# Gates and up-projections with the tokens stationary, the output projection in two halves of its k-tiles, and the memory pools moved to opposite ends

## The chip, the cores and the metric

One core of a Trainium2 chip runs the whole layer. Times are device microseconds of one execution; the profile is that of one execution of its own.

## What is computed

One decoder layer over 256 tokens of width 2048, in float32. A combined input projection feeds three attention branches (indexer-selected, block-gated, cross-attention into 256 memory tokens). Their outputs go through up-projections, are weighted by sigmoid gates, summed and projected; then come a layer norm, a mixture of 32 experts (two for each token), and a second layer norm.

```python
g_a, g_b, g_c = jnp.split(jax.nn.sigmoid(h @ w_gate[l] + b_gate[l]), 3, axis=-1)
merged = g_a * (o_a @ w_up_a[l]) + g_b * (o_b @ w_up_b[l]) + g_c * (o_c @ w_up_c[l])
x = layer_norm(ALPHA * x + merged @ w_o[l], ln1_g[l], ln1_b[l])
y = hier_moe(x, w_grp[l], b_grp[l], w_rt[l], b_rt[l], w1[l], w3[l], w2[l])
x = layer_norm(ALPHA * x + y, ln2_g[l], ln2_b[l])
```

`w_gate` is 2048 x 6144, `w_o` 2048 x 2048, and each of the 32 experts has three matrices of 2048 x 512.

## The kernel before

**Dense part.** `proj` (line 167) makes a list of units. A unit is one 128x512 (or two 128x256) piece of a weight matrix, 256 KB: `ld` loads it into one of six staging slots of `stt`, `sp` splits it on ScalarE and VectorE into a high and a low float32r part `wh`, `wl` (`split`, lines 147 and 148; three buffers), and `run` does three matmuls for each piece, high by high, high by low, low by high. `emit` (line 580) issues the load five units ahead and the split two units ahead. In the form "W" the weights stand in the array and the 256 tokens stream (12 matmuls of 256 columns a unit, lines 199 to 202; the result has channels on partitions). In the form "S" the tokens stand and the weights stream (6 matmuls of 512 columns, lines 207 to 209; the result has tokens on partitions). The instructions of an engine are put in an order by a scheduler, by when it reckons them ready.

The stages in order: input projections with the attention heads as filler between them, six gate stages of 32 units (form W, filler in the first three; `gate_evac` adds the bias, a value per partition, on ScalarE), 64 units of up-projections (W; `up_evac` multiplies by the gate, adds the branches and splits the sum into the tiles `mg`), 64 units of the output projection (S), over five column pieces `WO`, each over all 16 k-tiles. After a piece `residual_sum` adds it to the residual in `wx`, and `logit_step` transposes the sum and multiplies it with the router.

**Memory and stream.** `Stream` (line 636) loads the expert weights in slots of 2 MB. The first eight keys are loaded in halves: eight half-loads during the last gates, eight more at the units `WOL` of the output projection. After the dense part two further slots, `acc` and `yb`, open for one load each, and `wx` when the normalised rows have been taken from it. In the steady part `hidden` (line 987) uses four slots at a time and `used` gives them back, whereupon the next loads are issued on SyncE's queue.

**Tail.** The last group of four experts has its `w2` cut by output columns (`LAST`: 1024, 512, 512), so that the second norm can begin on the first columns. `load_ln2` spreads the norm's two rows over all partitions into the slot `main.ln` by 32 matmuls and eight ScalarE copies; it stands after the last group's `hidden`. Then comes a branch (`tc.If`), and in its `Else` the last slices (`last_slices`, line 1082) and `fast_tail` (line 1135), which prefills PSUM with the bias row, finishes the statistics and writes eight pieces of 128x512.

Of the kernel before, what the change touches and what calls it, by code (L numbers as in the profile page):

```python
# [8 lines left out]
F32 = mybir.dt.float32  # L9
# [40 lines left out]
def hybrid_trunk(ctx: ExitStack, tc: tile.TileContext, xp, xT, memT, w_mem_kv, w_in, gq, gkv, g_kidx, b_kidx,  # L50
# [21 lines left out]
    cs1 = ph1.enter_context(tc.tile_pool(name="cs1", bufs=1))  # L72
    gq_s = cs1.tile([P, 4], F32, name="gq_s")
    gkv_s = cs1.tile([P, 2], F32, name="gkv_s")
    bg_s = cs1.tile([P, 48], F32, name="bg_s")
# [9 lines left out]
    def load_consts():  # L85
# [4 lines left out]
        nc.sync.dma_start(bg_s, bg)  # L90
        nc.sync.dma_start(g1p, ln1_gp)
# [12 lines left out]
    xm = ph1.enter_context(tc.tile_pool(name="xm", bufs=4))  # L104
    wsp = ph1.enter_context(tc.tile_pool(name="wsp", bufs=3))
    wks = ExitStack()
    wk = wks.enter_context(tc.tile_pool(name="wk", bufs=2))
    k2 = ctx.enter_context(tc.tile_pool(name="k2", bufs=1, side="right"))
    slots = [k2.tile([P, W2D], F32, name=f"wk{i}") for i in range(NSK)]
    mos = ExitStack()  # L110
    g8 = mos.enter_context(tc.tile_pool(name="g8", bufs=6, side="right"))
    mo = mos.enter_context(tc.tile_pool(name="mo", bufs=4, side="right"))
# [37 lines left out]
    def act_tiles(pool, nm):  # L150
        ts = [pool.tile([P, 8, T], F32R, name=f"{nm}{n}", tag="a") for n in ("H0", "L0", "H1", "L1")]
        return Act(ts[0::2], ts[1::2], 8)
# [14 lines left out]
    def proj(src, c0, n, act, nkt, kind, evac, last=False):  # L167
# [7 lines left out]
        for u in range(nu):  # L175
            def ld(u=u):
                st = state["s", u] = stg()
                R["ld"] = nc.sync.dma_start(st[:, :kp * n].rearrange("p (k n) -> p k n", k=kp),
                                  src[u * kp * P:(u + 1) * kp * P, c0:c0 + n].rearrange("(k p) n -> p k n", p=P))
# [6 lines left out]
            def mm(u=u, cs=(0, 1)):  # L186
# [4 lines left out]
                for k in range(kp):  # L191
                    wh, wl = (t[:, k * n:(k + 1) * n] for t in state[u])
                    kt = u * kp + k
                    st_, sp_ = kt == 0, kt == nkt - 1
# [36 lines left out]
    A["x"] = act_tiles(xm, "x")  # L231
# [9 lines left out]
    wi = wk.tile([P, 2, NIH], F32, name="wi", bufs=1)  # L241
    later = []
# [125 lines left out]
    for k, i in enumerate(GO):  # L368
        proj_cols(w_gate, i * 1024, 1024, X, NKT, "W",
# [917 lines left out]
```

## Time and profile before

| what | us |
|---|---|
| median of 3 runs | 1702.85 (1702.12 to 1704.21) |
| the profiled execution's own time | 1701.77 |
| its span in the profile | 1700.0 |
| dense part, start to end of the output projection | 0 to 757 |
| routing and first gather | 757 to 767 |
| experts, up to the last weight's landing | 767 to 1673 |
| after the last landing | 1673 to 1700 |

The times in the profile count from the start of the span. Busy shares are of one engine; a matmul's duration in the profile is a latency, and what matmuls cost in a row is the distance from one start to the next.

### The profile page before, as it was taken

What the parts mean: (1) busy time and instruction counts of PE and PEld (TensorE: products, weight loads), DVE (VectorE), ACT (ScalarE), POOL (GpSimd) and SP (SyncE); (2) the same over time, 40 slices, a digit from 0 to 9 for tenths busy, and PEclk for the clock granted to TensorE, in tenths of its full rate; (3) what the DMA queues carried; (4) which work ended last, traced back from release to release, by engine and by line L of the source; (5) the groups of instructions that cost most, each with busy time, mean ns of one, the idle gap of its engine ahead of it and who ended that gap; (6) DMA issues with size and microseconds to landing.
All of it is one profiled execution on the core that took longest, in us unless ns stands there. A gap on an engine that the chain in (4) does not pass through costs nothing.

```text
span 1700.0 us, 23691 instructions
## 1 busy us (share of the span) xinstructions
PE 1472.8 (87%) x9489; PEld 956.8 (56%) x9489; DVE 596.2 (35%) x1126; ACT 465.0 (27%) x873; POOL 13.0 (1%) x24
## 2 busy tenths in 40 slices
PE   9999999999999999997976967877758768768677
PEld 8989989999999998883321222312212213222122
DVE  6656765565454676551120210200200101001004
ACT  5545455676545444441100000000000000000011
POOL 0000000000000000010000000000000000000000
PEclk9999999999999999998987978978979879879779
DMA  7766665555776667949999999999999999999994
GB/s 237 229 187 165 163 164 160 156 156 163 273 265 210 184 186 262 316 148 424 426 427 426 428 427 427 427 428 426 427 428 426 427 427 427 427 427 427 428 404 158
DMA packets 118279, 540.70 MB, mean 318 GB/s; under 512 B 13680, under 2 KB 27792, under 8 KB 93072
## 3 DMA queue, kind: packets, MB, share of 16 engines
q1 hardware_dynamic: 118160, 539.10, 82.8%
q8 instruction: 77, 1.26, 0.3%
q14 instruction: 42, 0.34, 0.1%
HBM read 536.95 MB, written 2.10 MB: 317 GB/s over the span
## 4 chain that ended last, share of the span: by engine, by line
PE 55%; DMA 41%; DVE 1%; ACT 1%; issue 1%; SPq 1%; POOL 0%; ACTq 0%; DVEq 0%; POOLq 0%
DMA wg<-in_w_dram 17%; DMA wk<-in_w_dram 15%; PE ps L202 10%; PE ps L199 10%; PE ps L201 10%; PE h L992 8%; DMA wkk<-in_w_dram 5%; DMA wx<-in_w_dram 4%; PE ps L208 3%; PE ps L207 3%; PE ps L209 3%; PE yp L1073 3%; PE yp L1096 1%; DMA stt<-in_w_o_dram 1%; SPq L704 1%
## 5 line engine op out<-in xcount | busy, mean ns | idle before, releaser
L148 DVE TENSOR_TENSOR wl<-stt,wh 128x512 fp32r<-128x512 f32 (+1 forms) x492 | 333.9, 684 | 264.1 <-ACT wh L147 260.5
L147 ACT CAST wh<-stt 128x512 fp32r<-128x512 f32 (+1 forms) x492 | 300.7, 615 | 311.1 <-PE ps L201 203.8
L992 PE MATMUL h<-wg,xg 128*32 128x512 f32 x912 | 240.4, 702 | 80.2 <-DMA wg<-in_w_dram 80.2
L199 PE MATMUL ps<-xH,wh 128*128 128x256 f32 x1024 | 293.7, 287 | 0.0
L202 PE MATMUL ps<-xH,wl 128*128 128x256 f32 x1024 | 289.7, 283 | 0.8 <-DVE wl L148 0.7
L201 PE MATMUL ps<-xL,wh 128*128 128x256 f32 x1024 | 289.7, 283 | 0.0
L992 PE MATMUL h<-wk,xg 128*32 128x512 f32 x688 | 201.9, 712 | 57.3 <-DMA wk<-in_w_dram 57.3
L199 PEld LDWEIGHTS ps<-xH,wh 128*128 128x128 f32 x1024 | 196.2, 192 | 1.6 <-issue 1.3
L202 PEld LDWEIGHTS ps<-xH,wl 128*128 128x128 f32 x1024 | 196.1, 192 | 1.5 <-DVE wl L148 1.5
L201 PEld LDWEIGHTS ps<-xL,wh 128*128 128x128 f32 x1024 | 196.3, 192 | 0.3
L963 DVE TENSOR_SCALAR xg<-gp,g1n,b1n 128x128 f32<-128x128 f32 x56 | 23.0, 410 | 428.2 <-PE h L992 375.3
L992 PEld LDWEIGHTS h<-wg,xg 128*32 128x32 f32 x912 | 53.1, 126 | 198.0 <-DMA wg<-in_w_dram 108.8
L992 PE MATMUL h<-wkk,xg 128*32 128x512 f32 x208 | 116.9, 718 | 18.3 <-DMA wkk<-in_w_dram 18.3
L992 PEld LDWEIGHTS h<-wk,xg 128*32 128x32 f32 x688 | 44.5, 128 | 148.7 <-DMA wk<-in_w_dram 83.0
L992 PE MATMUL h<-wx,xg 128*32 128x512 f32 x208 | 115.7, 710 | 12.1 <-DMA wx<-in_w_dram 12.1
L960 ACT ACTIVATE xg<-gp,b1n,g1n 128x128 f32<-128x128 f32 x56 | 25.6, 457 | 361.1 <-PE h L992 252.4
L1073 PE MATMUL yp<-wg,yb 128*32 128x512 f32 x368 | 95.8, 597 | 8.3 <-DMA wg<-in_w_dram 8.3
L1073 PE MATMUL yp<-wk,yb 128*32 128x512 f32 x304 | 87.2, 595 | 5.3 <-DMA wk<-in_w_dram 5.3
L1001 DVE COPY yb<-yp 128x512 f32<-128x512 f32 x15 | 10.4, 692 | 196.4 <-PE yp L1073 170.0
L202 PE MATMUL ps<-oH,wl 128*128 128x256 f32 x256 | 72.0, 281 | 0.0
L199 PE MATMUL ps<-oH,wh 128*128 128x256 f32 x256 | 71.7, 280 | 0.0
L201 PE MATMUL ps<-oL,wh 128*128 128x256 f32 x256 | 71.2, 278 | 0.0
(316 smaller groups left out, 1962.1 us busy)
## 6 DMA issues: line engine op xcount, KB each, us to landing
wg<-in_w_dram SPq DMA_DIRECT2D x76, 2048.0 KB, 27.6
wk<-in_w_dram SPq DMA_DIRECT2D x56, 2048.0 KB, 27.6
stt<-in_w_gate_dram SPq DMA_DIRECT2D x192, 256.0 KB, 2.9
wx<-in_w_dram SPq DMA_DIRECT2D x20, 2048.0 KB, 28.1
wkk<-in_w_dram SPq DMA_DIRECT2D x18, 2048.0 KB, 29.2
stt<-in_w_in_dram SPq DMA_DIRECT2D x104, 256.0 KB, 2.9
stt<-in_w_o_dram SPq DMA_DIRECT2D x64, 256.0 KB, 4.7
wk<-in_w_dram SPq DMA_DIRECT2D x14, 1024.0 KB, 10.1
```

What stands on the lines that cost most here:

```text
L147: nc.scalar.copy(h, src)
L148: nc.vector.tensor_tensor(l, src, h.bitcast(F32), ALU.subtract)
L199: nc.tensor.matmul(o, hb, a.H(kt), start=st_ and b % 2 == 0, stop=False, skip_group_check=True)
L201: nc.tensor.matmul(o, hb, a.L(kt), start=False, stop=False, skip_group_check=True)
L202: nc.tensor.matmul(o, lb, a.H(kt), start=False, stop=sp_, skip_group_check=True)
L207: nc.tensor.matmul(o, ha, wh, start=st_, stop=False)
L208: nc.tensor.matmul(o, ha, wl, start=False, stop=False)
L209: nc.tensor.matmul(o, la, wh, start=False, stop=sp_)
L960: nc.scalar.activation(xg[:, kt], gp[:, j], AF.Identity, scale=g1n[:, kt:kt + 1], bias=b1n[:, kt:kt + 1])
L963: nc.vector.tensor_scalar(xg[:, kt], gp[:, j], g1n[:, kt:kt + 1], b1n[:, kt:kt + 1], ALU.mult, ALU.add)
L992: nc.tensor.matmul(h[32 * e:32 * e + 32, :], xg[:, 8 * c + j, 32 * e:32 * e + 32], wt[e][:, j, :], start=(c == 0 and j == 0), stop=(c == 1 ...
L1073: nc.tensor.matmul(yps[n][32 * e:32 * e + 32, :], hT[:, 2 * k + j, 32 * e:32 * e + 32], wt[e][:, j, n * 512:(n + 1) * 512], start=(k + j = ...
```

## The change

- The gates and the up-projections take the form S. The gate's bias now lies along the free dimension: it is transposed once, written to a small DRAM tile `bgd`, and read back for each piece of 512 channels as 128 equal rows (`load_bias`, 12 loads on SyncE's queue into one buffer `bgb`). `gate_evac` does two VectorE adds a piece in place of four ScalarE activations. Since the merged result now has tokens on partitions, it is transposed (`turned`: four transposes and a split for each half of the tokens and each piece `s`).
- The output projection runs over k-tiles 0 to 7 for all five pieces, then over 8 to 15. `residual_sum` is called after either half.
- The activation tiles `x` and `mg` lie in two pools, `xma` and `xmb`, at one end of memory; the expert slots and what follows grow from the other end. `xma` closes after the first half of the output projection and its place becomes the slot `acc`; `xmb` closes after the second half and becomes `yb`, whose load is issued before the routing.
- The residual's rows are loaded earlier (`XL`), and two more half-loads are spread over the output projection (`WOL`, `HALVES`).
- `load_ln2` moves ahead, between the two input halves of the last group's `hidden`, into PSUM tiles of `py`. For this the slot `main.ln` is left out of the stream from the second half of that group on.
- In `fast_tail` two prefills stand before the last slices, one matmul and one ScalarE copy fall away, one VectorE operation comes in.

```diff
-HALVES = 8, 11, 15
+HALVES = 9, 11, 15
-WOL = (3, 8, 13, 18, 23, 28, 34, 41)
-XL = (1, 10, 20, 30, 39)
+WOL = (3, 9, 14, 20, 25, 31, 37, 43, 48, 53)
+XL = (1, 5, 12, 18, 22)
...
-    def gate_evac(ps, o, n, late):
-        t = gt[o // 1024]
-        for b in range(n // P):
-            blk = o // P + b
-            nc.scalar.activation(t[:, blk % 8, :], ps[b // 2][:, b % 2 * T:b % 2 * T + T], AF.Sigmoid if late else AF.Identity,
-                                 bias=bg_s[:, blk:blk + 1])
+    def gate_evac(ps, o, late):
+        t = by_chunk(gt[o // 1024])
+        for c in range(2):
+            d = t[:, c, o % 1024:o % 1024 + 512]
+            nc.vector.tensor_tensor(d, ps[c], bgb, ALU.add)
+            if late:
+                nc.scalar.activation(d, d, AF.Sigmoid)
+
+    def load_bias(o):
+        nc.sync.dma_start(bgb, bgd[o // P:o // P + 4, :].rearrange("a b -> (a b)").partition_broadcast(P))
...
-        proj_cols(w_gate, i * 1024, 1024, X, NKT, "W",
+        proj_cols(w_gate, i * 1024, 1024, X, NKT, "S",
...
+        def turned(c):
+            g0, m, o = gslice(0), mg["a"], (s % 2) * 4
+            tp = pa.tile([P, 4, P], F32, name=f"mt{s}{c}", tag="pa")
+            for k in range(4):
+                nc.tensor.transpose(tp[:, k, :], g0[:, c, k * P:(k + 1) * P], ident)
+            cs = slice(c * P, (c + 1) * P)
+            split(m.Ht[s // 2][:, o:o + 4, cs], m.Lt[s // 2][:, o:o + 4, cs], tp)
...
-            proj(wu, s * 512, 512, lambda b0=b0: OAct(b0), nk, "W", up_evac(br, s))
+            proj(wu, s * 512, 512, lambda b0=b0: OAct(b0), nk, "S", up_evac(br, s))
...
-    for i, (o, w, _) in enumerate(WO):
-        proj(w_o, o, w, lambda: mg["a"], NKT, "S", wo_evac(i), last=i == len(WO) - 1)
+    for half in range(2):
+        for i, (o, w, _) in enumerate(WO):
+            proj(w_o, o, w, lambda: mg["a"], NKT // 2, "S", wo_evac(i, half), half == 1 and i == len(WO) - 1, 8 * half)
...
-                if k[0] == "n":
+                if self.ln is not None and k[1] == NQ - 1 and (k[0] == "n" or k[2] == 1):
...
+        if k == (n7 - n6) // 2 - 1:
+            xms[0].close()
+            ap = ctx.enter_context(tc.tile_pool(name="ap", bufs=1, reuse_waits="tile"))
+            acc2 = ap.tile([P, W2D], F32, name="acc")
+            main.add([acc2], True)
...
+    xms[1].close()
+    yp_ = ctx.enter_context(tc.tile_pool(name="yb", bufs=1, reuse_waits="tile"))
+    yb2 = yp_.tile([P, W2D], F32, name="yb")
+    main.add([yb2], True)
...
     pp = pa.tile([P, 2, NE], F32, name="pos", tag="pa")
+    R["ld"] = None
+    main.load()
...
+                    if first and c == 0 and q == NQ - 1:
+                        load_ln2()
...
-                if i == 0:
-                    prefill(0, 0, PS["phh"].tile([P, 512], F32, name="w00", tag="h1"))
-                    prefill(1, 0, PS["phh"].tile([P, 512], F32, name="w10", tag="h3"))
                 return
             comb_(then=chain)
 
+        for c in range(2):
+            prefill(c, 0, PS["phh"].tile([P, 512], F32, name=f"w{c}0", tag=f"h{1 + 2 * c}"))
         go(after)
...
-        for c, i in ((0, 0), (0, 1), (1, 0), (0, 2), (1, 1)):
-            whole = i and c == 0
+        for c, i in ((0, 0), (0, 2), (1, 0), (1, 1), (0, 1)):
+            whole = (c, i) == (0, 1)
...
-        last_op(0, 0)
         first_op(1, 2)
-        last_op(1, 3)
-        for i in (1, 2):
-            V2(nc.scalar.copy(piece(0, i), ws[0, i]))
-            store(0, i)
-        last_op(1, 2)
-        last_op(1, 0)
-        last_op(1, 1)
+        for c, i in ((0, 0), (1, 3), (0, 2), (1, 2), (1, 0), (1, 1)):
+            last_op(c, i)
+        V2(nc.scalar.copy(piece(0, 1), ws[0, 1]))
+        store(0, 1)
 
     ln2 = [main.ln[:, :D], main.ln[:, D:]]
     go = moe_round(main, True)
-    load_ln2()
```

## Rows read from the trace of the kernel before

**Rows 1.** The page: the span, the busy time of the engines, and the mean busy share of the DMA engines in 40 slices of 42.5 us.

```profile
span 1700.0 us, 23691 instructions
PE 1472.8 (87%) x9489; PEld 956.8 (56%) x9489; DVE 596.2 (35%) x1126; ACT 465.0 (27%) x873; POOL 13.0 (1%) x24
DMA  7766665555776667949999999999999999999994
```

**Rows 2.** Busy time in six stretches: the last three gates, the up-projections, the output projection, the expert stream, the end of the stream, and what follows. Columns: the stretch, its length, busy us and instructions of PE, PEld, DVE, ACT, POOL; granted clock; DMA share; GB/s.

```profile
420.00:564.00 144.00, 144.00 (x1203) 144.00 (x1202) 72.71 (x109) 71.84 (x128) 0.00 (x0) 1.00 0.74 241
572.00:654.00 82.00, 82.00 (x698) 82.00 (x698) 63.07 (x91) 38.53 (x62) 0.00 (x0) 1.00 0.61 186
654.40:757.00 102.60, 101.02 (x575) 86.52 (x573) 55.84 (x97) 43.94 (x74) 1.55 (x3) 1.00 0.73 251
762.00:1650.00 888.00, 682.21 (x3682) 227.50 (x3680) 112.99 (x208) 51.76 (x105) 0.18 (x1) 0.87 1.01 426
1650.00:1673.00 23.00, 16.31 (x84) 5.24 (x85) 3.52 (x6) 0.75 (x2) 0.00 (x0) 0.75 0.89 322
1673.00:1700.00 27.00, 20.49 (x86) 7.01 (x84) 17.14 (x32) 3.92 (x9) 1.40 (x2) 0.98 0.21 78
```

**Rows 3.** PE's instructions in order of time, in a gate of form W; eight more stand between the two rows. Columns: start, duration, engine, line, operation, output and inputs, shapes.

```profile
509.81 0.28 PE L199 MATMUL ps<-xH,wh 128*128 128x256 f32 x1
...
510.89 0.28 PE L199 MATMUL ps<-xH,wh 128*128 128x256 f32 x1
```

**Rows 4.** The same, in an input projection of form S on the tile `x`; four more stand between the rows.

```profile
227.67 0.39 PE L208 MATMUL ps<-wl,xH 128*128 128x512 f32 x1
...
228.80 0.39 PE L207 MATMUL ps<-wh,xH 128*128 128x512 f32 x1
```

**Rows 5.** The same, in the memory's projection of form S on the tile `m`, which lies in another pool than `x`; four more stand between the rows.

```profile
99.76 0.40 PE L208 MATMUL ps<-wl,mH 128*128 128x512 f32 x1
...
100.92 0.40 PE L207 MATMUL ps<-wh,mH 128*128 128x512 f32 x1
```

**Rows 6.** ScalarE's instructions in order of time: the evacuations at the start and the end of 16 units of form S on `x` with attention as filler, and at the ends of two neighbouring pieces of 16 gate units of form W without filler.

```profile
225.81 0.59 ACT L305 ACTIVATE kb<-ps 128x512 f32<-128x512 f32 x1
250.82 0.59 ACT L312 COPY vb<-ps 128x512 f32<-128x512 f32 x1 [0.94 <-PE ps L209]
...
539.89 1.57 ACT L360 ACTIVATE g<-ps,bg_s 128x256 f32<-128x256 f32 x4 [0.22 <-PE ps L202]
562.93 1.57 ACT L360 ACTIVATE g<-ps,bg_s 128x256 f32<-128x256 f32 x4 [0.22 <-PE ps L202]
```

**Rows 7.** VectorE's instructions in order of time: the products at the end of the first and of the last of the twelve up-projections.

```profile
571.87 1.28 DVE L394 TENSOR_TENSOR g<-ps,g 128x512 f32<-128x512 f32 x2
...
653.84 1.28 DVE L394 TENSOR_TENSOR g<-ps,g 128x512 f32<-128x512 f32 x2
```

**Rows 8.** Groups of instructions by shape, in the up-projections. Columns: line, engine, operation, names, shapes, count, busy us, mean ns of one, idle of the engine before them and what ended it.

```profile
L148 DVE TENSOR_TENSOR wl<-stt,wh 128x512 fp32r<-128x512 f32 x58 | 40.0, 689 | 18.1 <-ACT wh L147 17.9
L394 DVE TENSOR_TENSOR g<-ps,g 128x512 f32<-128x512 f32 x23 | 14.8, 682 | 0.0
L398 DVE TENSOR_TENSOR g<-g,g 128x1024 f32<-128x1024 f32 x7 | 8.5, 1218 | 0.0
```

**Rows 9.** The chain that ended last, in the output projection: eight transposes (start, length, what).

```profile
730.74 0.87 PE xt L473 x8
```

**Rows 10.** The output projection: ScalarE's splits with the idle time before them, and the DMA issues (KB each, median us from issue to landing).

```profile
L147 ACT CAST wh<-stt 128x512 fp32r<-128x512 f32 x62 | 38.3, 621 | 48.4 <-PE ps L209 20.6 <-DMA stt<-in_w_o_dram 13.3 <-DVE wl L148 11.8
...
stt<-in_w_o_dram SPq DMA_DIRECT2D x56, 256.0 KB, 4.8
```

**Rows 11.** What the DMA engines moved from 735 to 775 us, in 40 slices of 1 us, and one issue in that stretch (us from issue to landing last).

```profile
GB/s 90 0 45 209 178 140 196 215 132 193 3 0 0 0 0 31 2 16 0 0 0 0 0 0 180 82 360 426 410 459 410 442 442 393 451 426 410 475 410 360
wx<-in_w_dram SPq DMA_DIRECT2D x1, 2048.0 KB, 15.1
```

**Rows 12.** SyncE's DMA issues in order of time, around the routing.

```profile
758.82 0.36 SPq L704 DMA_DIRECT2D acc<-in_w_dram  x1
...
762.21 0.33 SPq L704 DMA_DIRECT2D wx<-in_w_dram  x1
770.77 1.28 SPq L704 DMA_DIRECT2D wk<-in_w_dram  x3
```

**Rows 13.** The page's DMA issues: the slots of the steady stream.

```profile
wk<-in_w_dram SPq DMA_DIRECT2D x56, 2048.0 KB, 27.6
```

**Rows 14.** PE's instructions in order of time at the end: the transposes of the last group, the last row spread, the first and the last matmuls of the last slices. In brackets: idle time before, and what ended it.

```profile
1640.46 0.74 PE L1056 MATMUL ht<-ident,yb 128*128 128x128 f32 x4
...
1647.47 2.07 PE L925 MATMUL l2p<-rows,ident 32*128 32x256 f32 x4 [0.68 <-ACT wg L1108]
1654.46 1.07 PE L1096 MATMUL yp<-wk,yb 128*32 128x512 f32 x2 [4.92 <-issue]
...
1679.77 3.63 PE L1096 MATMUL yp<-wk,yb 128*32 128x512 f32 x30
```

**Rows 15.** The last weights: SyncE's last four loads, and the issues of that size from 1560 us on (median us to landing last).

```profile
1657.90 4.61 SPq L697 DMA_DIRECT2D wk<-in_w_dram  x4
...
wk<-in_w_dram SPq DMA_DIRECT2D x8, 512.0 KB, 10.7
```

**Rows 16.** VectorE's instructions in order of time, first and last of the final norm.

```profile
1688.45 1.40 DVE L1189 SCALAR_TENSOR_TENSOR acc<-acc,mv,wg 128x512 f32<-128x512 f32 x2
...
1695.88 0.75 DVE L1194 SCALAR_TENSOR_TENSOR acc<-acc,rs,w 128x512 f32<-128x512 f32 x1 [1.76 <-PE w L1180]
```

More of the change, by code (lines that the diff above doesn't have):

```diff
@@ L90, in load_consts, with turn @@
         nc.sync.dma_start(bg_s, bg)
+        def turn():
+            tp = pa.tile([P, 512], F32, name="bgt", tag="pa")
+            nc.tensor.transpose(tp[:48, :P], bg_s, ident)
+            nc.scalar.copy(bg_t, tp[:48, :P])
+            nc.sync.dma_start(bgd, bg_t)
+        later.append((20, turn))
         nc.sync.dma_start(g1p, ln1_gp)
@@ L101, in rsqrt_eps @@
         nc.gpsimd.tensor_tensor(dst, t, nhalf, ALU.pow)
-    xm = ph1.enter_context(tc.tile_pool(name="xm", bufs=4))
-    wsp = ph1.enter_context(tc.tile_pool(name="wsp", bufs=3))
+    wsp = ph1.enter_context(tc.tile_pool(name="wsp", bufs=3, side="right"))
+    xms = [ExitStack(), ExitStack()]
+    xmb, xma = (x.enter_context(tc.tile_pool(name=n, bufs=2, side="right")) for x, n in zip(xms[::-1], ("xmb", "xma")))
+    k2 = ctx.enter_context(tc.tile_pool(name="k2", bufs=1))
+    slots = [k2.tile([P, W2D], F32, name=f"wk{i}") for i in range(NSK)]
+    mos = ExitStack()
+    g8 = mos.enter_context(tc.tile_pool(name="g8", bufs=6))
+    mo = mos.enter_context(tc.tile_pool(name="mo", bufs=4))
     wks = ExitStack()
     wk = wks.enter_context(tc.tile_pool(name="wk", bufs=2))
[L108 to L112, printed above, removed]
     ps1 = ExitStack()
@@ L150, in act_tiles @@
     def act_tiles(pool, nm):
-        ts = [pool.tile([P, 8, T], F32R, name=f"{nm}{n}", tag="a") for n in ("H0", "L0", "H1", "L1")]
+        ts = [q.tile([P, 8, T], F32R, name=f"{nm}{n}", tag="a") for q, n in zip(pool, ("H0", "L0", "H1", "L1"))]
         return Act(ts[0::2], ts[1::2], 8)
@@ L241, in hybrid_trunk @@
     wi = wk.tile([P, 2, NIH], F32, name="wi", bufs=1)
+    bgb = wk.tile([P, 512], F32, name="bgb", bufs=1)
+    bg_s = wk.tile([P, 48], F32, name="bg_s", bufs=1)
+    bg_t = wk.tile([48, P], F32, name="bg_t", bufs=1)
     later = []
@@ L399, in ev @@
                 if br == 2:
-                    m = mg["a"]
-                    o = (s % 2) * 4
-                    split(m.Ht[s // 2][:, o:o + 4, :], m.Lt[s // 2][:, o:o + 4, :], g0)
+                    for c in range(2):
+                        later.append((2 + c, lambda c=c: turned(c)))
         return ev
@@ L424, in ev @@
         def ev(ps, cs=(0, 1)):
+            if half == 0:
+                for c in cs:
+                    residual_sum(i, c, ps[c], 0)
+                return
             if i + 1 == len(WO):
@@ L438, in hybrid_trunk, with residual_sum @@
     V = tc.keep_in_program_order
-    def residual_sum(i, c, ps):
+    def residual_sum(i, c, ps, half):
         _, w, kt = WO[i]
@@ L643, in __init__ @@
         def __init__(self, first):
-            self.i, self.slot, self.free, self.done, self.once = 0, {}, [], set(), set()
+            self.i, self.slot, self.free, self.done, self.once, self.ln = 0, {}, [], set(), set(), None
             u = []
@@ L729, in hybrid_trunk @@
     hooks[15] = load_consts
+    for k, i in enumerate(GO):
+        for h in range(2):
+            hooks[n4 + 32 * k + 16 * h + 9] = lambda o=i * 1024 + h * 512: load_bias(o)
     keep_warm(45)
@@ L852, in hybrid_trunk @@
     ph1.close()
-    accp = ctx.enter_context(tc.tile_pool(name="accp", bufs=1, reuse_waits="tile"))
-    acc2, yb2 = (accp.tile([P, W2D], F32, name=n) for n in ("acc", "yb"))
-    main.add([acc2, yb2], True)
     rt = ctx.enter_context(tc.tile_pool(name="rt", bufs=1, reuse_waits="tile"))
-    sct = rt.tile([P, 2, P], F32, name="sct")
     xgp = ctx.enter_context(tc.tile_pool(name="xgp", bufs=1, reuse_waits="tile"))
@@ L862, in hybrid_trunk @@
     xg = xgp.tile([P, NKT, P], F32, name="xg")
-    rows = rt.tile([32, 256], F32, name="rows")
+    xsf = R["xs"].rearrange("p a b -> p (a b)")
+    rows = xsf[:32, 256:512]
     R["ld"] = None
```

55 lines of the change are left out of this document (27 added, 28 removed).

## The prediction

> **What bounds the kernel.** I read the busy time by stretch first, because the averages of the page hide that two different engines set the pace [rows 1]. Up to 757 us TensorE is the bound: in the gates and the up-projections it is busy all the time at the full granted clock, while the DMA engines are at 0.61 to 0.74 [rows 2]. From 762 to 1650 us the DMA engines are at 1.01 and move 426 GB/s, and TensorE waits [rows 2]. The reader is to see that in the first part a microsecond off TensorE's work is a microsecond off the time, and that in the second part nothing counts but when the stream starts and how many bytes are then left. In the last 50 us the stream is over and TensorE and VectorE follow one another; there TensorE is late: the last weights are issued at 1657.90 + 4.61 us at the latest and land some 10.7 us after issue, at about 1672.6 [rows 15], but the last matmuls on them run until 1679.77 + 3.63 = 1683.4 [rows 14]. So there are three places to gain, and they add: the dense part, the start of the stream, the tail.
>
> **Gates, form W to form S.** Nine steps of form W take 1.08 us, 0.120 each, or 1.44 us for a unit of twelve [rows 3]; two evacuations 16 units apart, at 539.89 and 562.93, give the same 1.44 [rows 6]. Form S on the same tile takes 1.13 us for five steps, 0.226 each, 1.36 us for a unit of six [rows 4]; on the tile `m` it is 0.232, 1.39 us [rows 5]. Which holds after the pools have moved I can't see; tile `x` and the weight buffers stay neighbours, so I take 1.36. There are 192 gate units: 192 x 0.08 = 15.4 us less, with 9.6 us as the lower bound (1.39) and, if a step could be as much shorter as `m` is longer (0.220), 23 us as the upper one. The filler costs what it did: 16 units of form S with filler took 25.0 us [rows 6], 21.7 of it for the units.
>
> The fixed part of a step is what is saved, six of them a unit. The Trainium skill (TensorE: Matmul & The Clock Gate, section Back-to-back issue gap) puts a warm step at N/2.4 + 2.5 ns, so that halving the number of steps would save an estimated 15 ns a unit, 2.9 us in the gates. The rows disagree with it (0.120 against 0.109, 0.226 against 0.216); I go by the rows.
>
> The evacuation is off TensorE: two VectorE adds of 0.68 us for a PSUM piece [rows 8] in place of four ScalarE activations. VectorE does 72.7 us of work in 144 [rows 2], so they fit, and there are two units of lead. The bias loads are 12 of 256 KB beside 48 MB of gate weights, at a DMA share of 0.74: nothing.
>
> **Up-projections.** The products of the first and the last projection start at 571.87 and 653.84, 58 units apart: 1.413 us a unit [rows 7]. The attention outputs lie where `m` lay, so I take 1.39 for form S: 64 x 0.023 = 1.5 us less; the other bound is 1.36, 3.4 us less. Added are 32 transposes, eight in 0.87 us [rows 9]: 3.5 us. Net 2.0 us more (bounds 0.1 and 2.0). VectorE gets tight: after the second branch's evacuation (2 x 0.68 + 1.22) come four units with 0.69 each, 5.3 us of work [rows 8] in 4 x 1.39 = 5.6 us of matmuls, and the new split follows on it. Late next would be `wl`. I put 1 us in the sum (bounds 0 and 5: four times the 1.3 us of lead).
>
> **Output projection.** The same matmuls in another order; ten residual additions, five of them new, on a VectorE that works 55.8 of 102.6 us [rows 2]. ScalarE's splits waited 13.3 us for `w_o` tiles here, which land 4.8 us after issue with the prefetch beside them [rows 10]. The first half now carries the residual rows and six half-loads: 8.4 + 2.1 + 6.3 = 16.8 MB, 39 us at 426 GB/s under 44 us of matmuls. I put 0.5 us (bounds -1 and 3).
>
> **Start of the stream.** Before, `acc`, `yb` and `wx` are issued from 758.82 to 762.21 [rows 12], after some 15 us in which next to nothing moves [rows 11], and the last of them lands at 762.21 + 15.1 = 777.3 [rows 11]; the slots freed by the first matmuls, issued from 770.77 on [rows 12], wait behind that. After the change two of the three are in already. `wx` is still held until the rows are normalised, and alone it is through 4.9 us after its start, at about 769. Then the queue is empty until 770.77 plus about 1.5 us (data of the issue of 758.82 flow from about 760 on [rows 11]): 772.3. All eleven slots are full in either case, so the gain is not the 4 MB (9.8 us) but 777.3 - 772.3 = 5.0 us; bounds 3 and 7.
>
> **Tail.** Before, the last row is spread until 1647.47 + 2.07 = 1649.5, then TensorE sits 4.92 us for nothing that the profile shows, and the last slices begin at 1654.46, long after their first weights have landed [rows 14]. With `load_ln2` moved ahead, the last work before the branch is the transposes, over at 1641.2 [rows 14]; with the same 4.92 us the slices begin at 1646.1. From there to the end of the last slice it took 1683.4 - 1654.5 = 28.9 us, which would give 1675.0; the last landing at 1672.6 and half of the 3.63 us that the last slice takes give about the same. I take 1676: 7.4 us less (bounds 0 and 9). The 32 matmuls and eight copies go into a gap in which TensorE waits for weights. The slot left out costs nothing while the queue is deep: a load lands 27.6 us after its issue [rows 13], some five slots of 4.9 us; with one slot less it is over 20 us.
>
> The 4.92 us follow a branch. The Trainium skill (Runtime: NRT & Kernel Launch, section Instruction fetch mechanics) says that a taken branch forces its target page to be fetched first; that agrees, and by it the wait would stay, only earlier.
>
> In the final norm VectorE's nine long operations, with a wait of 1.76 us for TensorE before the last, end at 1696.6 [rows 16]; ten at 0.70 to 0.75 without that wait end at about 1695.7: 1 us less.
>
> **The sum.** -15.4 + 2.0 + 1.0 + 0.5 - 5.0 - 7.4 - 1.0 = -25.3. The profiled execution took 1701.8 us (its span is 1700.0), 1.1 us below the median of the runs shown: 1676.5, or 1677 to 1678 beside the median. I predict 1677.
>
> **Rivals.** (1) The tail doesn't come forward, since the branch or the fetching of its code, not the rows spread, sets the start; two idle stretches in the slices speak for it, the landing of their weights against it. Then 1677 + 7.4 = 1684. (2) The dense part gains little. With steps of 0.232 in the gates it is 1683, with VectorE late in the up-projections up to 1687: chance 0.10. If a step cost by its columns alone, 0.240 for 512 after 0.120 for 256, the gates would gain nothing, 1692: chance 0.03, since no row of form S is that long (0.226 and 0.232 [rows 4, 5]). The skill's rule named above lies near this case: by its estimate of 2.9 us it would be about 1689. (3) More than reckoned: 0.220 a step and 7 us at the stream's start, 1667. (4) Slower: SyncE's queue. Each bias load has one buffer and waits until the piece before has been evacuated, and behind it the gate weights wait. A staging ring of six units is 8 us, of which a load and its split use about half; a hold of more than 4 us plus 25.3/12 = 2.1 us on each of the twelve would eat everything and turn the sign: with 9 us each, 12 x 5 = 60 us more than forecast, 1737. Against it: VectorE is free half the time, and the evacuated piece is ready a unit or two before SyncE comes to that load.
>
> **How the numbers follow.** As forecast 0.61 (own range 1671 to 1682), rival 1 0.14, rival 2 0.10 and 0.03, rival 3 0.07, rival 4 0.04, and 0.01 for a hold on SyncE's queue that just takes the gain back. Measurements of this kernel can't tell less than about 0.2%, 3.4 us, from no change; faster than that is 0.95, slower 0.04. The range 1666 to 1689 leaves out rival 4 and the far ends of rivals 2 and 3.
>
> **What would show it.** Matmuls of 512 columns in the gates 0.226 apart and gate evacuations 21.7 us apart; up-projections 91 to 94 us long; `yb` issued at the end of the output projection and no dip of the DMA share to zero but for some 3 us before the stream; the first matmul of the last slices some 5 us after the last group's transposes; the last slice's matmuls ending within 4 us of the last landing; the stream still at 426 GB/s. Wrong would make it: steps of 0.232 or idle time of TensorE before `wl` in the gates, idle time of TensorE behind SyncE's bias loads, or a gap in the stream in the last group, where one slot is missing.

## The result, and the profile after

The changed kernel takes 1680.2 us (median of 4 runs, 1680.0 to 1680.4), the one before 1703.5 (median of 4): a ratio of 0.9864, 95% interval 0.9847 to 0.9881, or 23.3 us less. 1677 was predicted, with a range of 1666 to 1689. The profiled execution has a span of 1678.6 us against 1700.0 [rows 1]. The page of the changed kernel, the lines for the span, the engines and the DMA share in 40 slices of 42 us:

```profile
span 1678.6 us, 20715 instructions
PE 1458.4 (87%) x7984; PEld 878.5 (52%) x7984; DVE 615.0 (37%) x1165; ACT 456.0 (27%) x841; POOL 12.6 (1%) x24
DMA  7766565555887558959999999999999999999996
```

TensorE has 1505 instructions fewer, but is busy only 14.4 us less. The same six stretches as in [rows 2], each moved by what the kernel had gained up to there (length; busy us and instructions of PE, PEld, DVE, ACT, POOL; granted clock; DMA share; GB/s):

```profile
409.30:553.30 144.00, 143.49 (x629) 117.29 (x628) 83.13 (x127) 71.97 (x119) 0.00 (x0) 1.00 0.78 258
562.60:644.60 82.00, 82.00 (x366) 66.10 (x365) 61.53 (x91) 38.33 (x63) 0.00 (x0) 1.00 0.58 181
645.00:747.30 102.30, 101.71 (x583) 87.50 (x581) 60.44 (x108) 44.56 (x75) 1.46 (x3) 1.00 0.79 273
753.50:1637.60 884.10, 678.37 (x3679) 224.33 (x3679) 111.93 (x202) 51.04 (x104) 0.00 (x0) 0.87 1.00 424
1637.60:1660.60 23.00, 22.26 (x135) 6.18 (x137) 10.89 (x18) 1.17 (x2) 0.00 (x0) 0.93 0.88 312
1660.60:1678.60 18.00, 11.53 (x36) 4.37 (x28) 10.12 (x21) 2.75 (x7) 1.41 (x2) 0.99 0.35 117
```

The kernel is still bound as before, by TensorE at the full granted clock first and by the DMA engines at 1.00 then. New are 0.51 us without work for TensorE in the gates (before: none; a record lasts 0.39 us at a pitch of 0.227, so that of each wait only what is over 0.16 us shows as idle), and that what follows the stream is 18 us long and not 27.

To place the gain, the run is cut at six events: ScalarE's last copy into `vb`, the first evacuation of the last gate piece, the first product of the last up-projection, the start of the last `ps` matmul of the output projection, the landing of the first weights in a slot that the first expert matmuls have freed, and the last weight landing. Lengths in us of the profiled execution:

| stretch | before | changed | difference | forecast |
|---|---|---|---|---|
| start to `vb` | 264.39 | 265.39 | +1.0 | 0 |
| gates | 298.54 | 286.92 | -11.6 | -15.4 |
| up-projections | 90.91 | 92.18 | +1.3 | +3.0 |
| output projection | 102.48 | 102.17 | -0.3 | +0.5 |
| to the first freed slot's weights | 23.51 | 20.78 | -2.7 | -5.0 |
| from there to the last landing | 892.78 | 892.77 | 0.0 | 0 |
| last landing to the end | 27.35 | 18.40 | -8.95 | -8.4 |
| sum | 1700.0 | 1678.6 | -21.4 | -25.3 |

The first line can't be put down to the change: in the nine experiments that keep its code there, the stretch was 263.7 to 266.1 us long. The forecast of the last line is the tail and the final norm together. Each length is that of one execution. In the experiments that keep the code and the loads of a stretch, the gates took 285.4 to 288.0 us, the up-projections 92.1 to 92.2, the output projection 101.6 to 103.9, the stretch to the first freed slot 19.4 to 20.8 and the last one 18.4 to 18.5. So the tail's gain is sure to a tenth of a microsecond, those of the gates and of the stream's start only to one or two.

**Gates.** TensorE's instructions in order of time in the last gates, six steps apart:

```profile
509.81 0.39 PE L217 MATMUL ps<-wh,xL 128*128 128x512 f32 x1
...
511.17 0.39 PE L217 MATMUL ps<-wh,xL 128*128 128x512 f32 x1
```

VectorE's evacuations of the last two gate pieces, in order of time:

```profile
530.55 1.28 DVE L374 TENSOR_TENSOR g<-ps,bgb 128x512 f32<-128x512 f32 x2
552.31 1.28 DVE L374 TENSOR_TENSOR g<-ps,bgb 128x512 f32<-128x512 f32 x2
```

A unit takes 1.36 us, 16 of them 21.76, exactly the forecast price against 23.04 before [rows 6]. But of the last six pieces only three took 21.76; the others took 22.1 to 22.9 us.

**Start of the stream.** SyncE's issues in order of time, from the output projection's end on:

```profile
746.97 0.34 SPq L733 DMA_DIRECT2D yb<-in_w_dram  x1
...
752.60 0.34 SPq L733 DMA_DIRECT2D wx<-in_w_dram  x1
762.24 1.28 SPq L733 DMA_DIRECT2D wk<-in_w_dram  x3
```

What the DMA engines moved from 730 to 770 us, in 40 slices of 1 us:

```profile
GB/s 252 238 61 0 0 0 8 16 0 0 0 0 0 0 0 0 0 82 197 311 377 459 459 330 277 344 459 442 401 107 16 0 0 164 287 418 434 418 434 418
```

The first load into a freed slot, issued at 762.24 (KB, us from issue to landing):

```profile
wk<-in_w_dram SPq DMA_DIRECT2D x1, 1024.0 KB, 5.2
```

`acc` is issued at 714 and 721 us, `yb` at the end of the output projection, and the DMA engines are idle for some 3 us before 763, as foreseen. Not foreseen is that they are idle for longer ahead of that: from 733 to 747 us their share is 0.01, as it was from 745 to 758 in the kernel before [rows 11], since the last of `w_o` is in by then and no load of expert weights is issued between the second half of `acc` and `yb`. Where the load of 770.77 took 9.1 us to land, behind 6 MB, this one takes 5.2.

**Tail.** TensorE in order of time: the last group's transposes, the first of the early products, the first and the last slices (in brackets idle time before, and what ended it):

```profile
1628.85 0.74 PE L1096 MATMUL ht<-ident,yb 128*128 128x128 f32 x4 [0.85 <-DVE yb L1091]
1635.76 3.75 PE L1188 MATMUL w<-wg,ident 128*128 128x512 f32 x4 [6.17 <-issue]
1639.44 1.07 PE L1136 MATMUL yp<-wkk,yb 128*32 128x512 f32 x2
...
1658.33 3.83 PE L1136 MATMUL yp<-wk,yb 128*32 128x512 f32 x30
```

Two windows of the same stretch (columns as above), at the early products and in the slices:

```profile
1635.70:1640.30 4.60, 4.54 (x9) 1.38 (x13) 0.00 (x0) 0.00 (x0) 0.00 (x0) 0.50 1.04 371
1641.40:1652.00 10.60, 10.60 (x76) 2.98 (x72) 2.76 (x5) 0.59 (x1) 0.00 (x0) 1.00 1.01 344
```

The wait behind the branch is still there, 6.17 us, but it begins right behind the transposes, at 1629.6; before, it began 8 us behind them, when the last row was spread [rows 14]. The last slice ends 1.95 us behind the last landing at 1660.21; before it was 10.8.

### The profile page after: what moved, and what is told of

Its sections match the earlier page's. It is cut to its first block, busy times and chain, and to the rows that moved or that the text cites. A ratio compares the mean times of both kernels' runs of the same rounds, so it can differ in the third digit from the quotient of the medians.

```text
span 1678.6 us, 20715 instructions
## 1 busy us (share of the span) xinstructions
PE 1458.4 (87%) x7984; PEld 878.5 (52%) x7984; DVE 615.0 (37%) x1165; ACT 456.0 (27%) x841; POOL 12.6 (1%) x24
## 4 chain that ended last, share of the span: by engine, by line
PE 54%; DMA 42%; DVE 1%; issue 1%; ACT 1%; SPq 1%; POOL 0%; ACTq 0%; DVEq 0%; POOLq 0%
DMA wg<-in_w_dram 15%; DMA wk<-in_w_dram 15%; PE ps L216 10%; PE ps L217 9%; PE ps L215 9%; PE h L1030 9%; DMA wkk<-in_w_dram 5%; DMA wx<-in_w_dram 4%; PE yp L1113 3%; PE ps L210 3%; PE ps L207 3%; PE ps L209 3%; DMA stt<-in_w_gate_dram 1%; PE yp L1136 1%; DMA stt<-in_w_o_dram 1%
## 5 line engine op out<-in xcount | busy, mean ns | idle before, releaser
L1030 PE MATMUL h<-wg,xg 128*32 128x512 f32 x896 | 230.2, 703 | 74.3 <-DMA wg<-in_w_dram 74.2
L215 PE MATMUL ps<-wh,xH 128*128 128x512 f32 (+2 forms) x512 | 198.1, 389 | 0.3 <-ACT wh L155 0.2
L216 PE MATMUL ps<-wl,xH 128*128 128x512 f32 (+2 forms) x512 | 195.3, 381 | 2.9 <-DVE wl L156 2.8
L217 PE MATMUL ps<-wh,xL 128*128 128x512 f32 (+2 forms) x512 | 194.8, 381 | 0.0
L1001 DVE TENSOR_SCALAR xg<-gp,g1n,b1n 128x128 f32<-128x128 f32 x56 | 22.9, 410 | 424.9 <-PE h L1030 373.6
L998 ACT ACTIVATE xg<-gp,b1n,g1n 128x128 f32<-128x128 f32 x56 | 25.6, 457 | 356.5 <-PE h L1030 252.5
L216 PEld LDWEIGHTS ps<-wl,xH 128*128 128x128 f32 x512 | 96.7, 189 | 22.6 <-DVE wl L156 5.4
L215 PEld LDWEIGHTS ps<-wh,xH 128*128 128x128 f32 x512 | 96.3, 189 | 18.3 <-ACT wh L155 1.6
L217 PEld LDWEIGHTS ps<-wh,xL 128*128 128x128 f32 x512 | 96.6, 189 | 17.4
L1039 DVE COPY yb<-yp 128x512 f32<-128x512 f32 x15 | 10.4, 691 | 189.9 <-PE yp L1113 173.0
L207 PE MATMUL ps<-xH,wh 128*128 128x256 f32 x256 | 73.3, 286 | 0.0
L210 PE MATMUL ps<-xH,wl 128*128 128x256 f32 x256 | 72.7, 284 | 0.2 <-DVE wl L156 0.2
L209 PE MATMUL ps<-xL,wh 128*128 128x256 f32 x256 | 72.6, 284 | 0.0
## 6 DMA issues: line engine op xcount, KB each, us to landing
wx<-in_w_dram SPq DMA_DIRECT2D x20, 2048.0 KB, 27.1
```

Of the source, the lines that this page charges most:

```text
L207: nc.tensor.matmul(o, hb, a.H(kt), start=st_ and b % 2 == 0, stop=False, skip_group_check=True)
L209: nc.tensor.matmul(o, hb, a.L(kt), start=False, stop=False, skip_group_check=True)
L210: nc.tensor.matmul(o, lb, a.H(kt), start=False, stop=sp_, skip_group_check=True)
L215: nc.tensor.matmul(o, ha, wh, start=st_, stop=False)
L216: nc.tensor.matmul(o, ha, wl, start=False, stop=False)
L217: nc.tensor.matmul(o, la, wh, start=False, stop=sp_)
```

## Experiments

Each kernel is the changed one with the edit shown. Where a stretch is given, it is one of the table's.

**The gates and up-projections back in the old form.** (`e2_w_form`: the bias goes back to ScalarE's activations, the sum to its split without transposes.)

```
-        proj_cols(w_gate, i * 1024, 1024, X, NKT, "S",
+        proj_cols(w_gate, i * 1024, 1024, X, NKT, "W",
...
-            proj(wu, s * 512, 512, lambda b0=b0: OAct(b0), nk, "S", up_evac(br, s))
+            proj(wu, s * 512, 512, lambda b0=b0: OAct(b0), nk, "W", up_evac(br, s))
```

> The changed kernel with gates and up-projections back in form W, the bias a value per partition on ScalarE, no transposes of the merged result; the memory's places, the halves of the output projection and the tail stay as changed. Theory (the gain of the dense part is the steps' fixed cost): gate pieces without filler 23.0 us apart instead of 21.8, the gates 11 to 12 us longer, the up-projections 1 us shorter, the input part 1 us shorter (no turned bias), together 9 to 12 us slower than 1680.2, about 1691. Rival (the new places in memory made the matmuls quicker, not the form): the gates keep 21.8 us a piece and the time stays within 2 us of 1680.2.

Measured: 1690.4 us (1687.0 to 1691.8), ratio 0.9922 (0.9902 to 0.9943). Gates 298.60, up-projections 90.91, both as in the kernel before to 0.1 us; from the output projection on, the stretches lie where those of the other kernels lie (18.41 us behind the last landing). So the new places in memory didn't make the matmuls quicker. The form is worth 11.7 - 1.3 = 10.4 us beside this trace of the changed kernel (9.4 to 12.0 with the gates' spread above), and the rest of the change about the other half.

**No prefetch beside the gates.** (`e5b_no_prefetch`: the eight loads of 1 MB that are issued during the last three gates wait for later slots.)

```
-            if n >= LATE and k % 8 == 4 and main.i < PRE:
+            if n >= LATE and k % 8 == 4 and main.i < 0:
```

> The changed kernel without the eight half-loads of expert weights during the last three gates (they are loaded later, so the time as a whole is longer by what 8 MB cost in the stream, up to 20 us, about 1699). The gates alone are looked at. Theory (the last three gates miss 2 us of their gain because gate weights land late behind a 1 MB load): all six pieces of the last three gates 21.8 us apart, the three gates together 130.6 to 131.2 us instead of 132.7. Rival (VectorE or the bias loads hold TensorE): 132 us or more.

Measured: 1683.1 us, ratio 0.989 (0.9871 to 0.991). Five of the last six gate pieces take 21.76 us, one 22.06: 130.86 together and not 132.74. In the nine kernels that keep the gates and their prefetch, the changed one among them, the six take 131.2 to 133.8 us, so this one lies below them all, and the waits in the gates come with the prefetch. The price is paid at the stream: the first freed slot's weights land 26.61 us behind the output projection, not 20.78, and the last ones 892.2 us after them. The time of about 1699 that was expected did not come: the span is 3.0 us longer than the changed kernel's and not 19. The later loads found room where the changed kernel's DMA engines are idle, at the end of the output projection (from 730 to 744 us: share 0.88, 357 GB/s).

**The prefetch in quarters.** (`e8_quarters`: the same bytes in the same stretch, each 1 MB load as four of 256 KB, two units apart.)

```
-                main.load()
+                main.load_now(parts)
+            if parts and k % 2 == 0:
+                with tc.issue_after(R["ld"].ins):
+                    nc.sync.dma_start(*parts.pop(0))
```

> The eight prefetched weight loads beside the last three gates (1 MB each) are issued in quarters of 256 KB, two units of the gates apart. Theory (the gates wait since a gate weight load is stuck behind 1 MB): the last three gates take 130.6 to 131.3 us in place of 132.7, the whole of the gates 285 to 286, and the time comes 1 to 2 us down, 1678 to 1679.5. Rival (it is the DMA share, not the size of one load, that makes the gate weights late): 132.2 to 133.5 us again and the same time.

Measured: 1677.2 us (1676.7 to 1678.8), ratio 0.9862 (0.9846 to 0.9878); the last six gate pieces take 130.85 us, the gates 285.00. DMA issues of a stretch of 20 us in the gates (KB each, median us from issue to landing) in the changed kernel:

```profile
stt<-in_w_gate_dram SPq DMA_DIRECT2D x15, 256.0 KB, 5.7
wk<-in_w_dram SPq DMA_DIRECT2D x2, 1024.0 KB, 7.9
```

The same stretch with quarters:

```profile
stt<-in_w_gate_dram SPq DMA_DIRECT2D x15, 256.0 KB, 3.7
wk<-in_w_dram SPq DMA_DIRECT2D x8, 256.0 KB, 4.1
```

The same 2 MB of prefetch are issued in both windows, and the gate weights land 2 us sooner with quarters, though the DMA share of the window is higher (0.88 against 0.80): it is the size of the load ahead of them that makes them late, not the share. Over all gate loads of the last three gates the medians are closer, 4.2 us and 3.8; what falls is the longest, from 8.5 to 5.9 us, and to 4.3 without prefetch. The quarters are smaller and also spread out, two units apart; the two weren't tried one by one. By its trace this version gains 1.9 us in the gates on the changed kernel, and 0.35 on the best of the nine kernels with whole loads; the ratios of 0.9862 and 0.9864 can't tell it from the changed kernel.

**`acc`, then `acc` and `yb`, opened later in the program.** (`e3_acc_late`, `e3b_both_late`: both loads stand behind the output projection in the text, in the second behind the routing's start. Both kernels also go back to eight half-loads in the output projection, so that `acc` is one load of 2 MB.)

```
-            main.add([acc2], True)
...
-    main.add([yb2], True)
+    main.add([acc2, yb2], True)
```

> The changed kernel with the slot acc opened only after the output projection, together with yb, both issued as whole loads ahead of the routing; eight half-loads in the output projection as before. Theory (the stream's start is set by when the first slots come back, about 762 us; between the end of the output projection at 747 and then both slots and wx, 6.3 MB or 14.8 us, just fit): within 1 us of 1680.2, so that the halves of the output projection bring next to nothing. Rival (each slot that is filled earlier saves its 4.9 us, or the 2.8 us measured at the stream's start come from acc): 2.5 to 5 us slower, 1683 to 1685.

> The changed kernel with acc and yb both issued after the routing's logits, as before the change; eight half-loads in the output projection. Theory (issuing before the routing what can be issued there is the whole gain at the stream's start): from the end of the output projection to the last weight's landing 916 to 917 us, as before the change (916.3), where the changed kernel has 913.6 and the one with acc opened late 914.3. Rival (half-loads or places in memory shortened the stream): 914.5 us or less.

Measured: 1679.6 and 1678.8 us, ratios 0.9865 (0.9847 to 0.9883) and 0.9867 (0.9848 to 0.9887). No difference, but the edits didn't do what they were for: in both traces `acc` is issued at 715 and 716 us and `yb` at 746 and 747, since an issue goes out when its memory is free, not where it stands in the text. The two runs say nothing about the start of the stream, and the theory that the second would be slower could not be tried with them.

**`acc` and `yb` held behind `wx`.** (`e3c_held`: the loads keep their slots, but are ordered behind the issue of `wx`; eight half-loads again.)

```
     main.add([wx])
     main.load()
+    with tc.issue_after(R["w"].ins):
+        for k, half in held:
+            main.issue(k, half)
```

> acc and yb are issued only behind wx (at about 753 us), and not at 713 to 747 as in the changed kernel; the weights are the same, in the same slots. In the kernel before, the changed one and the run without prefetch, the stretch from the first landing of a freed slot's weights to the last landing of all was 892.8, 892.8 and 892.2 us. Theory (the stream ends a fixed time after the first of the freed slots is filled): wx lands at about 761, acc and yb by about 771, the first freed slot's weights at 773 to 774 in place of 767.4, and the last landing and the time come 5.5 to 7 us later than in the changed kernel: 1685 to 1688. Rival (4 MB more or less at the stream's start are hidden, since the queue is deep anyway): the last landing stays 913 to 915 us behind the output projection's end, and the time within 2 us of the changed kernel's.

Measured: 1686.2 us (1684.1 to 1687.1), ratio 0.9909 (0.9893 to 0.9926). SyncE's issues in order of time:

```profile
753.03 0.35 SPq L739 DMA_DIRECT2D wx<-in_w_dram  x1
753.43 0.42 SPq L739 DMA_DIRECT2D acc<-in_w_dram  x1
753.90 0.42 SPq L739 DMA_DIRECT2D yb<-in_w_dram  x1
762.63 1.28 SPq L739 DMA_DIRECT2D wk<-in_w_dram  x3
```

The first load into a freed slot, issued at 762.63:

```profile
wk<-in_w_dram SPq DMA_DIRECT2D x1, 1024.0 KB, 11.5
```

It lands 27.06 us behind the output projection, 6.3 later than in the changed kernel, and the last weights land 892.07 us after it. That is 3.6 us later than in the kernel before, too, where `acc` and `yb` went out 3 us ahead of `wx` [rows 12]: the run shows what 4 MB in front of the first freed slot cost, not the change's own gain. In all 13 traces of this case that last length lies between 892.1 and 894.0 us, while the one before it goes from 19.4 to 27.1. So the stream ends a fixed time, to within 2 us, after its first freed slot is filled, and what delays that delays the end: by 6.3 us there and by 5.6 at the last landing in this run, both counted from the output projection's end.

**The tail's parts put back.** `e1_rows_back`: the rows are spread behind the last group again, through the old PSUM tiles. `e1b_prefill_back`: the two first products of the final norm go back from ahead of the last slices to between the first and the second of them. `e1c_tail_back`: both. `e1d_whole_tail`: both, the old rule for the reserved slot and the old order of the final norm.

```
-                    if first and c == 0 and q == NQ - 1:
-                        load_ln2()
...
     go = moe_round(main, True)
+    load_ln2()
```

> The changed kernel with one part undone: the second norm's rows are spread behind the last group again, into the two PSUM tiles of before; the prefills and the final order stay as changed. Theory (the 32 matmuls and eight copies ahead of the branch made TensorE late in the tail): the last slices begin some 13 us after the last group's transposes instead of 6, their last matmul ends 9 to 11 us after the last weight has landed instead of 2, and the time is 7 to 9 us longer than the changed kernel's 1680.2, about 1688. Rival (the prefills ahead of the slices, or the branch itself, set it): the last matmul still ends within 3 us of the last landing, the time stays within 1.5 us of 1680.2. The dense part and the stream stay as they are by either.

> The changed kernel with only the two prefills put back between the first and the second of the last slices. Theory (the tail is now paced by the last weights' landing, so TensorE has room for 1.9 us of prefills): the last matmul of the slices ends 2 to 3 us after the last landing, as in the changed kernel (1.95), and the span ends 18 to 19.5 us after it (changed: 18.4). Rival (the prefills are the rest of the gain that putting the rows back did not take away): the last matmul 3.5 to 5.5 us after the last landing, the span 20 to 22 us after it.

> The changed kernel with both undone, the rows spread behind the last group and the prefills between the slices; only the final order of the norm stays changed. Theory (these two carry the whole gain of the tail): the last matmul of the slices 10 to 11 us after the last landing, as before the change (10.8), and the span 26.5 to 27.5 us after it (before 27.4, changed 18.4). Rival (the final order carries 1 us or more of it, as forecast): the span 26.4 us or less after the last landing though the last matmul is as late as before.

> As the run with rows and early products put back, and the rule for the reserved slot and the order of the final norm put back too: the whole tail in the form of the kernel before, the rest in the new form. There it was 24.9 us from the last weights' landing to the end, and in the kernel before 27.4; the records of the kernel before have two idle stretches of TensorE with no releaser among the last slices (4.9 us ahead of them, 2.2 us at 1660.28), the run with two parts put back only the first. Theory: the missing 2.4 us are the second stretch and belong to these two remaining edits, so that it is back and 27.0 to 27.7 us are measured, with TensorE's last slices 28 to 29 us long. Rival: the second stretch comes from something outside the tail (where the code lies), and it is 24.5 to 25.5 us again, with slices of 25 to 26 us. Both: a time some 6 to 9 us above that of the changed kernel.

| kernel | median, ratio (interval) | last landing to last slice's end | to the end |
|---|---|---|---|
| before | | 10.79 | 27.35 |
| changed | 1680.2, 0.9864 (0.9847 to 0.9881) | 1.95 | 18.40 |
| early products back | 1682.3, 0.9886 (0.9867 to 0.9906) | 1.95 | 18.40 |
| rows back | 1683.8, 0.9896 (0.9876 to 0.9916) | 7.40 | 23.90 |
| both back | 1684.9, 0.9903 (0.9878 to 0.9928) | 8.40 | 24.91 |
| whole tail back | 1685.7, 0.9905 (0.9889 to 0.9922) | 8.58 | 25.77 |

In the kernels that keep the whole tail the last length is 18.40 to 18.54 us, so these differences stand clear of the noise. The rows spread are 5.5 us; the early products alone are nothing (the 2 us in their median lie ahead of the tail: in the trace the output projection already ends 1.4 us later than in the changed kernel) and 1.0 us where the rows are late; the last two edits are another 0.86. That leaves 1.6 us of the 8.95 that no undone edit brought back. Of the four expectations only that for the early products held. With the rows back the last slice ended 7.40 us behind the last landing, where 9 to 11 were expected, or at most 3 by the rival; with both back it was 8.40 and not 10 to 11; with the whole tail the end came 25.77 us behind the last landing and not 27.0 to 27.7, with slices 25.6 us long as the rival had them (its end, 24.5 to 25.5, is just missed). Windows of the last slices in the kernel before (columns as above):

```profile
1654.40:1657.90 3.50, 3.44 (x11) 0.65 (x12) 0.00 (x0) 0.00 (x0) 0.00 (x0) 0.50 1.06 383
1657.90:1660.20 2.30, 0.16 (x1) 0.00 (x0) 0.00 (x0) 0.00 (x0) 0.00 (x0) 0.96 0.95 315
1660.20:1662.40 2.20, 2.12 (x16) 0.72 (x19) 0.00 (x0) 0.00 (x0) 0.00 (x0) 0.80 1.01 358
1662.40:1665.00 2.60, 2.60 (x17) 0.81 (x13) 0.00 (x0) 0.00 (x0) 0.00 (x0) 0.52 1.04 385
```

The same with both parts back:

```profile
1641.00:1646.00 5.00, 4.95 (x24) 1.38 (x28) 0.00 (x0) 0.00 (x0) 0.00 (x0) 0.50 1.03 337
1646.00:1652.00 6.00, 6.00 (x54) 1.72 (x46) 0.69 (x1) 0.58 (x1) 0.00 (x0) 1.00 1.00 350
```

The kernel before has a second idle stretch among its last slices, 2.22 us that wait for nothing the profile shows, and behind it the granted clock falls again, to 0.80 and 0.52 in the two windows, that is, to the lower of the two levels (1.2 GHz) for most of the second. With both parts back there is one stretch at 0.50, behind the 4.9 us after the branch, and then 1.00. The second stretch came back in none of the four kernels, not with the whole tail as before either; the last slices take 25.6 us there and took 28.9 before. What in the rest of the change took it away stays open.

**The bias without its turn.** (`e4_bias_direct`: the bias rows come in row order from memory; no transpose, no store and no second load through `bgd`.)

```
-        later.append((20, turn))
...
-        nc.sync.dma_start(bgb, bgd[o // P:o // P + 4, :].rearrange("a b -> (a b)").partition_broadcast(P))
+        nc.sync.dma_start(bgb, bg[o // P:o // P + 4, :].rearrange("a b -> (a b)").partition_broadcast(P))
```

> The changed kernel with the gate's bias taken row by row from an input laid out in rows, so that the transpose, its copy and the store to DRAM near 46 us fall away; the twelve loads of bias rows stay. Theory (the store holds SyncE's queue and sets the input part back by 1.1 us): the first evacuation of the cross-attention queries at 72.3 instead of 73.4 us and everything after it 1 us earlier, 1679. Rival (the 1.1 us are the new places in memory): no change, 1680.2.

Measured: 1679.9 us, ratio 0.9865 (0.9844 to 0.9886), start to `vb` 264.93 against 265.39. Inconclusive: the same stretch differs by 2.4 us between kernels with the same code there. The first evacuation that the expectation names came at 72.77 us against 73.44, but at 71.6 to 74.2 in the nine experiments with the changed code, so that the 1.1 us it set out from lie within that spread.

## Why the prediction was right

The time came out 3 us above the forecast and inside its own range, by the mechanisms it named; the gates and the stream's start gave less than reckoned, the up-projections and the tail more. The sum is better than its terms: three lines of the table miss by 7.1 us to the one side, three by 3.1 to the other, and that they partly cancel is luck.

- **Gates, -15.4 forecast, -11.6 measured.** The price of a unit was right to the last digit (1.36). What failed is the multiplication by all 192 units. In the last 96 it gave 5.7 us and not 7.7: with units of 1.36 us the staging ring of six is 8.2 us, and the gate weight right behind a 1 MB load takes 5.8 to 8.5 from issue to landing, so TensorE waits for `wl`. The prediction has no term for that; it looked at the DMA share of 0.74 and not at the longest load ahead in the queue. Idle time before `wl` in the gates was one of its own signs of being wrong, and it came, if small: 0.45 us show as idle, some 2 are lost. The Trainium skill (DMA: Bandwidth & Descriptors, section Two DMAs through the same engine are not ordered) says that within one queue of a DMA engine descriptors start in order; the longest landings, 8.5 us with whole loads in the queue and 5.9 with quarters, agree with that. In the first 96 units, with attention as filler, it gave 5.9 us and not 7.7, in every kernel alike, though TensorE is busy all the time there. Half of that 1.8 us can be placed: leaving out the 31 that are longer than 0.26 us, the distances from one gate matmul to the next are 0.2284 us in the mean there and not 0.2267, which is 0.9 us over 515 of them. Why, and the other half, stays open.
- **Up-projections, +3.0 forecast, +1.3 measured.** Steps of form S are 0.233 us apart in the mean, as on `m`, so that 64 units cost 1.3 us less than before; the 24 transposes in the stretch add 2.6 us from start to start. Of the 1.7 us too many, one is the microsecond for VectorE, which fell away, as TensorE has no idle time there; the rest are the last eight of the 32 transposes, which the forecast counted here and which fall into the output projection's stretch.
- **Output projection, +0.5 and -0.3.** The same within what such a stretch varies (101.6 to 104.1 in the runs), with eight transposes more in it. `w_o` tiles land 6.0 us after issue, with `acc` beside them, and TensorE waits 0.4 us for `wl` in all.
- **Start of the stream, -5.0 and -2.7.** The mechanism is the forecast's: not the 4 MB but the time at which the freed slots begin to fill. Two sizes were off. From the issue of the first freed slot to the landing of its 1 MB the forecast comes to 1.5 us and 2.5 (1 MB at 426 GB/s), and 5.2 were needed; and that issue came 15.6 us after the output projection and not 14.5, which goes from 14.4 to 15.9 among the 13 kernels. How much of the 2.7 us is `acc`'s and how much `yb`'s no run separates. One sign failed: the DMA share was to fall to zero for some 3 us only, and it does so for 14 more at the end of the output projection.
- **Tail, -7.4 and -8.8; final norm, -1.0 and -0.1.** Rival 1 is out: the tail came forward with the rows, and the branch's wait went with it. The last slice now ends 1.95 us behind the last landing; the forecast had half of 3.63 there. By that it came to 1674.4 and by the slices' start to 1675.0, and put down 1676: the extra 1.4 us is what it kept back. Only the path by the landing was right. The slices start 9.85 us behind the transposes and not 4.92, since the wait is 6.17 us long and the early products come first, and they take 22.7 us and not 28.9, which held the second idle stretch of the kernel before; that these two errors leave only 1.3 us is luck. The slot left out of the stream cost nothing, as forecast: the stretch to the last landing is 892.77 us, and 892.13 with the old rule back. In the final norm VectorE ends 11.7 us behind the last slice and not 13.2, more than forecast, but from there to the end of the span it takes 4.7 us in place of 3.3: one product now goes through ScalarE's copy last, and its store is issued behind seven others. With the old order back, the end came 0.7 us later.
- **The other rivals.** A step by columns alone is out (0.227), and so is the other end, 0.220; the estimate of 2.9 us for the gates, from a formula that its section gives for a lone matmul, stands against 11.6. VectorE isn't late in the up-projections. SyncE's bias loads hold up nothing: `bgb` lands in 3.5 to 4.4 us, no evacuation waits for it, and without the prefetch, the bias loads in place, five of the last six gate pieces take 21.76 us.

## What to carry to other kernels

When matmuls get cheaper, work out anew how long the staging ring lasts against the longest landing of a tile that stands behind a large prefetch; splitting the prefetch into loads of the tile's own size, spread out, gave the waits back here, at the same bytes. Look also for stretches in which the DMA engines have nothing to do: eight prefetches left for later filled one here and cost some 3 us, not the 20 that their bytes take at 426 GB/s. Where a stream is bound by bandwidth, find the event from which its length is constant, and count only what comes ahead of it. Work in front of a branch puts off the wait behind the branch too, so move it to where TensorE waits anyway: 32 small matmuls and eight copies were worth 5.5 us here.

## What was unexpected of the hardware

- The pitch of form S went with the tile and not with its end of the memory: 0.227 us in the mean on `x` and on the merged result, 0.233 on `m` and the attention outputs, though the two pools changed ends. On `x` beside the filler it was 0.228. Why wasn't tried.
- From the first freed slot's landing to the last weights the stream took 892.1 to 894.0 us in 13 kernels, under tails and prefetches of several kinds.
- Behind the branch TensorE stood idle 4.8 to 6.3 us, and what it did first ran at 0.50 of the clock: pairs of matmuls 0.85 us apart, 0.43 once the clock was back. The early products fill just that time in the changed kernel.
- Kernels with the same code up to there differ by up to 2.4 us by the end of the input projections, more than several of the edits studied here are worth; only lengths of stretches could tell those apart.
